# Output projection of a gated decoder layer: token-major in seven products, and the embedding projection moved ahead of the MLP

## The chip, the cores and the metric

One core of a Trainium2 chip. The metric is device time in microseconds (us) of one execution; "before" is the median of three runs, 952.14 us (951.76 to 952.27).

## The reference

One layer over 512 tokens with D = 1024: a normed input projection, gated linear attention and dilated attention side by side, then the part that matters here. Everything is float32.

```python
mix = (jax.nn.sigmoid(g_gla) * y_gla + jax.nn.sigmoid(g_att) * y_att) @ w_out[i]
x = x + mix
h2 = rmsnorm(x, ln2[i])
x = x + jnp.square(jax.nn.relu(h2 @ w_mlp1[i])) @ w_mlp2[i]
h3 = rmsnorm(x, ln3[i])
x = x + jax.nn.sigmoid(h3 @ w_pg[i]) * (p[i] @ w_pp[i])
return rmsnorm(x, ln_f)
```

`y_gla` ends with a product with `w_o_gla`; `p[i]` is a per-layer embedding, 512 tokens x 256, and `p[i] @ w_pp[i]` depends on nothing else in the layer.

## The kernel before

**Numbers and tiles.** Each float32 operand is split into a rounded part `hi` (ScalarE, a copy into float32r, `split_hi`) and a residual `lo` (VectorE, `split_lo`), and each 128 x 128 block of a product is three matmuls: hi x hi, hi x lo, lo x hi (`three`, L336). Tiles of 128 x 512 come from one pool of `NU` buffers: `u` (float32) and `ur` (hi or lo of an operand). PSUM has four banks `mmt` and four banks `smt`.

**Weights.** Every weight piece is 128 x 1024 (512 KB) and is one entry of `OPERANDS`, in the order of use. `fetch` (L301) runs ahead of TensorE: it issues the loads three operands ahead (`prepare`, L245: SyncE loads, and GpSimd a DMA that adds a second piece onto it in SBUF, L250), forms weight sums on VectorE (`sums`, L258), rounds to `hi` on ScalarE (L319) and takes the residual `lo` on VectorE (L297). At most `NRAW` = 8 raw pieces, five `hi` and four `lo` are held.

**Products.** A plain feature-major tile (`fm`, L346) is 8 K blocks x 3 = 24 matmuls of 512 columns. Most large products are done in Strassen-Winograd form: the two operands are cut in 2 x 2 blocks, and seven products of sums of blocks replace eight. `strassen` (L374) does so feature-major with 256 columns, `wide` (L416) token-major with 512: for each of the seven `WIDE` stages (weight sum A11, S1, S2, A12, S3, S4, A22 against operand sum B11, T1, T2, B21, T3, B22, T4) 24 matmuls into two of the banks. `begin` copies a bank out when a quarter's first part is ready, `end` adds the last part.

**Order.** Instructions stand on each engine in the order in which the Python code emits them. `run` (L330) emits n matmuls and then calls `step` (L220), which emits one pending closure of the list `later`, and from time to time a step of a generator in `side`. So vector and scalar work is woven between the matmuls, and a matmul that comes too early waits for it.

**The stages around the change.** `fm("og.j")` makes eight feature tiles of `y_gla` (L1276); VectorE multiplies by the gate and adds the attention branch into `tb[j]`, which is split into `mix[j]`. `fm("wo.j", mix)` makes eight feature tiles of the output projection (L1365), and VectorE adds each onto the transposed residual `xx[j]`, loaded by GpSimd (L1289, L1367). `x1_tile` scales by `ln2`, squares and sums for the norm, and forms the seven operand sums of the first MLP product. `stats` sums over partitions with one-column matmuls (L498), `to_tokens` turns `xx` into token-major tiles `x2` with 32 transposes (L1310, L1314); both run as `side` work during the first MLP product. The MLP is `m1q0` to `m1q7` (`strassen`, L374) and then `m2_plain` and `m2_seven`, which accumulate onto `x2` (L1455). `last_inputs` (L1498) loads the transposed embedding and ln_f when the S3 products of `m2_seven` end. Behind the MLP come `pp0`, `pp1` (`tmaj`, L353: 48 matmuls of 512 columns, copied out by ScalarE, L1577), the norm (L485, L486), and the gate `pg0`, `pg1`, which starts with token tile 0 and ends with the final norm and the stores.

Of the kernel before, what the change touches and what calls it, by code (L numbers as in the profile page):

```python
# [10 lines left out]
F32 = mybir.dt.float32  # L11
# [37 lines left out]
def weight_units():  # L49
# [39 lines left out]
    fm("wo", "w_out", 0, 8)  # L89
# [6 lines left out]
    for j in range(2):  # L96
        u.append((f"pp{j}.0", "tm", "w_pp", 0, j * 512))
# [56 lines left out]
def early():  # L154
    after_wide = False
    for n, i in OPERAND.items():
# [20 lines left out]
NU, NW, PIECE, WAYS = 67, 5, 8, 2  # L177
# [6 lines left out]

NWARM = 9
# [3 lines left out]
def block_kernel(ctx, tc, xT, ws, pT, wts, wha, wa2, vec, lnf, rel, onehot, ident_d, mask_d, out):  # L189
    nc = tc.nc  # L190
    V, S, TE, SY, GP = nc.vector, nc.scalar, nc.tensor, nc.sync, nc.gpsimd

    const = ctx.enter_context(tc.tile_pool(name="const", bufs=1))
# [64 lines left out]
    def sums(i):  # L258
        q, _, what = OPERANDS[i].partition(".")
        if q.startswith("m2c"):  # L260
# [40 lines left out]
    def fetch(upto):  # L301

        while done[0] < min(upto, len(OPERANDS) - 1):
            i = done[0] = done[0] + 1
            if i >= 0:
# [6 lines left out]
                if q.startswith("m2c") and what[:2] == "S2" and f"{q}.S4{what[2:]}" not in S4_LOADED:  # L312
# [33 lines left out]
    def fm(name, rhs, off=0, w=None, ps=None):  # L346
# [3 lines left out]
        run(three(ps, [(cols(w, slice(off + i * P, off + (i + 1) * P)), rhs[i]) for i in range(len(rhs))]))  # L350
        return ps

    def tmaj(name, n, lhs, evac, tts=range(4)):  # L353
# [3 lines left out]
        for tt in tts:  # L357
            ps = mmt()
            mms = three(ps, [(lhs(k, tt), cols(ready[f"{name}.{k // 2}"], slice((k % 2) * 512, (k % 2 + 1) * 512)))
                             for k in range(2 * n)])  # L360
            if tt < 3:
                run(mms)
            else:
                for i in range(n):
                    run(mms[6 * i:6 * i + 6])
# [50 lines left out]
    def wide(name, xo, finish):  # L416
# [4 lines left out]
        def begin(m, t, n, b):  # L421
            def go():
                sums[m, t, n] = u32()
# [6 lines left out]
        for i, (op, xname, b) in enumerate(WIDE):  # L430
# [3 lines left out]
            for pr in range(4):  # L434
# [8 lines left out]
                run(mms, 3, shared=True)  # L443
# [3 lines left out]
            if i in WEND:  # L447
                (m, t), b = WEND[i]
                later.extend(end(m, t, n, b) for n in range(2))
# [57 lines left out]
    def rms_gen(acc, res, wait=0, gap=0, squared=False):  # L507
# [15 lines left out]
        bc = const.tile([P, T], F32, tag="rstd", name="rstd", bufs=2)  # L523
# [751 lines left out]
    mix = [None] * KC  # L1275
    for j in range(KC):  # L1276
        py = fm(f"og.{j}", og)
        V.tensor_tensor(ga[j], py, ga[j], op=OP.mult)
        V.tensor_tensor(tb[j], tb[j], ga[j], op=OP.add)  # L1279
        if j < KC - 1:  # L1280
            split_later(tb[j], mix, j)
        else:
            mix[j] = split(tb[j])
    drain()

    xx = []
    for j in range(KC):
        t = u32()
        GP.dma_start(t, xT[j * P:(j + 1) * P, :])  # L1289
        xx.append(t)  # L1290

    acc1, norm2 = [], []
    x2 = {}

    def stats():
        for _ in range(30):
            yield
        r = rms_tok(acc1[0], True)
        n = const.tile([P, 4], F32, name="nrm2")
# [3 lines left out]
    def to_tokens():  # L1303
        for m in range(2):
            for t in range(2):
                pts = [smt() for _ in range(2)]
                for n in range(2):
                    tok = slice((2 * t + n) * P, (2 * t + n + 1) * P)
                    for i in range(4):
                        TE.transpose(pts[n][:, i * P:(i + 1) * P], xx[4 * m + i][:, tok], ident)  # L1310
                yield
                for n in range(2):
                    x2[m, t, n] = u32()
                    S.activation(x2[m, t, n], pts[n], AF.Copy)  # L1314
                yield

    blk, xop = [None, None], {}
    def operand(name, g, x):
        xop[name, g] = split(x)

    def x1_tile(j):

        x, c = xx[j], cv[:, C_LN2 + j:C_LN2 + j + 1]
        g, p, k = j // 4, j % 4 // 2, j % 2

        def first():
            if blk[g] is None:
# [419 lines left out]
```

## Time and profile before

| | |
|---|---|
| median of three runs | 952.14 us |
| profiled execution, its own time | 951.71 us |
| its span, first to last instruction | 949.6 us |
| TensorE matmuls (PE) | 941.3 us busy, 5892 records |
| VectorE (DVE) / ScalarE (ACT) / GpSimd (POOL) | 726.5 / 540.8 / 102.9 us busy |
| last matmul ends, after the span's start | 942.6 us |
| read from HBM / written | 143.03 MB / 8.17 MB |

The page lists for each engine its busy time, its share of the span and its instructions. A group's row reads: line, engine, operation, output <- inputs by tile names, shapes, count | busy us, mean ns of one | idle time of the engine just before them and what ended it. The rows of the chain are: start in us from the span's start, us, what. A timeline row is: start, us, engine, line, operation, tiles, shape, count. A matmul's own duration overlaps the next one's, so the pace is the distance from start to start. Lines after the change are those of the changed kernel.

### The profile page before, as it was taken

The numbers are of one execution on the slowest core, as the hardware profiler recorded it, in microseconds if no ns is written. First come the engines' busy times: TensorE is split into PE (matmuls) and PEld (weight loads), VectorE is DVE, ScalarE is ACT, GpSimd is POOL, SyncE is SP. The second block draws the span as 40 slices with busy tenths as digits, with TensorE's granted clock in tenths as the row PEclk, the third lists the DMA queues.
The fourth block names the chain that finished last, engine by engine and source line by source line (L and its number), as shares of the span: only waits on it lengthen the run. The fifth ranks groups of instructions, "written<-read, shape, count | busy, mean of one in ns | idle before, by whom it ended". The sixth has DMA issues, their size and how long they took to land.

```text
span 949.6 us, 15089 instructions
## 1 busy us (share of the span) xinstructions
PE 941.3 (99%) x5892; PEld 849.4 (89%) x5892; DVE 726.5 (77%) x1029; ACT 540.8 (57%) x880; POOL 102.9 (11%) x143
## 2 busy tenths in 40 slices
PE   9999999999999999999999999999999999999997
PEld 8789998899988888999988889999999888888886
DVE  7698879866789589878855788677777788988554
ACT  7357546445675479775732448555566445555643
POOL 0150010120100012022020000001000010020000
PEclk9999999999999999999999999999999999999999
DMA  9474482973818466456563436655647546796102
GB/s 352 142 236 114 129 201 68 289 234 100 200 46 227 159 144 182 132 134 200 156 199 92 131 89 173 154 142 134 162 129 191 141 100 166 218 306 222 53 0 89
DMA packets 46022, 150.34 MB, mean 158 GB/s; under 512 B 6723, under 2 KB 7311, under 8 KB 45952
## 3 DMA queue, kind: packets, MB, share of 16 engines
q1 hardware_dynamic: 29664, 100.61, 31.1%
q0 software_dynamic: 12608, 44.26, 23.5%
q10 hardware_dynamic: 3680, 4.51, 1.3%
q8 instruction: 46, 0.75, 0.3%
q14 instruction: 24, 0.20, 0.1%
HBM read 143.03 MB, written 8.17 MB: 159 GB/s over the span
## 4 chain that ended last, share of the span: by engine, by line
PE 98%; issue 1%; DMA 0%; ACT 0%; DVE 0%; POOLq 0%; POOL 0%; DVEq 0%
PE mmt L333 78%; PE smt L333 10%; PE mmt L581 2%; PE smt L1015 2%; PE smt L955 1%; PE smt L878 1%; PE smt L848 0%; PE smt L972 0%; PE smt L961 0%; PE smt L847 0%; PE smt L971 0%; PE smt L1310 0%; PE smt L1171 0%; PE smt L1071 0%; DMA cv<-in_vec_dram 0%
## 5 line engine op out<-in xcount | busy, mean ns | idle before, releaser
L333 PE MATMUL mmt<-ur,hi 128*128 128x256 f32 (+1 forms) x2320 | 476.0, 302 | 0.0
L333 PEld LDWEIGHTS mmt<-ur,hi 128*128 128x128 f32 x2320 | 373.1, 188 | 16.6
L333 PE MATMUL mmt<-ur,lo 128*128 128x256 f32 (+1 forms) x1160 | 351.2, 303 | 0.0
L297 DVE TENSOR_TENSOR lo<-w,hi 128x1024 fp32r<-128x1024 f32 x248 | 302.1, 1221 | 56.9 <-PE mmt L333 35.9
L319 ACT ACTIVATE hi<-w 128x1024 fp32r<-128x1024 f32 x248 | 259.2, 1054 | 93.8 <-PE mmt L333 24.5
L333 PE MATMUL mmt<-hi,ur 128*128 128x512 f32 (+3 forms) x832 | 241.1, 374 | 0.0
L333 PEld LDWEIGHTS mmt<-ur,lo 128*128 128x128 f32 x1160 | 218.6, 188 | 8.2
L333 PEld LDWEIGHTS mmt<-hi,ur 128*128 128x128 f32 x832 | 150.3, 188 | 25.7
L333 PE MATMUL mmt<-lo,ur 128*128 128x512 f32 (+3 forms) x416 | 154.8, 372 | 0.0
L461 ACT ACTIVATE ur<-u 128x512 fp32r<-128x512 f32 x111 | 66.1, 624 | 87.2 <-DVE u L1279 30.9
L333 PEld LDWEIGHTS mmt<-lo,ur 128*128 128x128 f32 x416 | 78.2, 188 | 13.6
L297 DVE TENSOR_TENSOR ur<-u,ur 128x512 fp32r<-128x512 f32 x110 | 72.7, 688 | 11.8 <-ACT ur L461 9.5
L333 PE MATMUL smt<-hi,ur 128*128 128x512 f32 x256 | 79.1, 390 | 0.0
L454 DVE TENSOR_TENSOR u<-u,mmt 128x512 f32<-128x512 f32 (+1 forms) x88 | 54.2, 647 | 26.9 <-PE mmt L333 26.6
L401 ACT ACTIVATE u<-mmt 128x512 f32<-128x512 f32 x72 | 43.1, 598 | 52.6 <-PE mmt L333 52.5
L250 POOL DMA_DIRECT2D w<-in_wts_dram x42 | 40.2, 1001 | 246.1 <-DMA w<-in_wts_dram 94.0
L333 PEld LDWEIGHTS smt<-hi,ur 128*128 128x128 f32 x256 | 47.8, 188 | 9.8
L276 POOL DMA_DIRECT2D w<-in_wts_dram x18 | 16.1, 894 | 317.9 <-DVE w L273 156.9
L333 PE MATMUL smt<-lo,ur 128*128 128x512 f32 x128 | 49.8, 389 | 0.0
L1389 ACT ACTIVATE u<-u 128x512 f32<-128x512 f32 x24 | 15.0, 628 | 26.7 <-DVE u L1385 26.7
L333 PEld LDWEIGHTS smt<-lo,ur 128*128 128x128 f32 x128 | 24.0, 188 | 5.0
L1250 ACT ACTIVATE u<-u 128x256 f32<-128x256 f32 x32 | 11.4, 411 | 20.9 <-DVE u L454 20.9
(235 smaller groups left out, 838.1 us busy)
## 6 DMA issues: line engine op xcount, KB each, us to landing
w<-in_wts_dram SPq DMA_DIRECT2D x180, 512.0 KB, 4.7
w<-in_wts_dram POOLq DMA_DIRECT2D x64, 512.0 KB, 6.8
u<-in_xT_dram SPq DMA_DIRECT2D x8, 256.0 KB, 5.3
u<-in_ws_dram SPq DMA_DIRECT2D x8, 256.0 KB, 5.4
v_dram<-u ACTq DMA_DIRECT2D x8, 256.0 KB, 6.6
u<-v_dram POOLq DMA_DIRECT2D x8, 256.0 KB, 6.2
y_dram<-u ACTq DMA_DIRECT2D x8, 256.0 KB, 2.0
u<-y_dram POOLq DMA_DIRECT2D x8, 256.0 KB, 6.2
```

The source lines that it names most:

```text
L250: GP.dma_start(w, wts[UNIT[b]], accum_op=OP.add)
L276: GP.dma_start(w, wts[UNIT[f"{q}.A21"]], accum_op=OP.add)
L297: V.tensor_tensor(lo, x, hi.bitcast(F32), op=OP.subtract)
L319: S.activation(hi[:, s], w[:, s], AF.Copy, scale=1.0 if c is None else c)
L333: TE.matmul(o, lhsT=l, rhs=r, start=a, stop=b, skip_group_check=shared)
L401: S.activation(sums[c], bank[b], AF.Copy, scale=-scale if c[0] else scale)
L454: V.tensor_tensor(out, s, ps, op=OP.subtract if m else OP.add)
L461: S.activation(hi, x, AF.Copy)
L581: TE.matmul(q0ps[i], lhsT=(hi, hi, lo)[j][:, c], rhs=(xh, xl, xh)[j], start=not k and not j, stop=k == KC - 1 and j == 2)
L1015: TE.matmul(o, lhsT=l[a][:, lc], rhs=r[b], start=start and i == 0, stop=stop and i == 2)
L1250: S.activation(outs[n], s[:, halves(n)], AF.Sigmoid)
L1389: S.activation(s, s, AF.Square)
```

## The change

The output projection `w_out` becomes token-major and goes through `wide` in seven products, with the gated mix as the operand that the sums are made of: `mix_even` and `mix_odd` form T1, T2, T4 and T3 tile by tile while the `w_o_gla` tiles are made, and split them. Its weight units become `quadw` pieces; S4 is made by a DMA that adds A12 onto S2 in SBUF (L319), as in the second MLP product. The residual x is read token-major: `begin_x` copies a bank to `x2` and has GpSimd add the x rows by DMA (L1378, L1379); the two tiles of the last product are loaded plainly (L1383). `onto_x` adds the final part. `x1_parts` transposes the `x2` tiles back to features (32 transposes, L1412) with ln2 applied in the copy out of PSUM (L1420); `x1_splits` forms and splits the operands of the MLP. The norm is taken from row sums of squares (L1392). `pp0` and `pp1` follow directly, and SyncE stores their eight tiles in DRAM (L1482, L1483); `last_inputs` reads them back (L1621). The gate then follows the MLP at once, with the token tiles in the order 2, 3, 0, 1. `NU` is 68 instead of 67.

```diff
-    fm("wo", "w_out", 0, 8)
+    quadw("wo", "w_out", (0, 512))
+    for j in range(2):
+        u.append((f"pp{j}.0", "tm", "w_pp", 0, j * 512))
...
-            EARLY.setdefault(i - 2, []).append((n, f"{q}.A11.{what[3:]}", f"{q}.A21.{what[3:]}"))
+            EARLY.setdefault(i - (5 if q == "wo" else 2), []).append((n, f"{q}.A11.{what[3:]}", f"{q}.A21.{what[3:]}"))
...
+        elif q == "wo" and what[:3] == "S4.":
+            return
...
-                if q.startswith("m2c") and what[:2] == "S2" and f"{q}.S4{what[2:]}" not in S4_LOADED:
+                if (q == "wo" or q.startswith("m2c")) and what[:3] == "S2." and f"{q}.S4{what[2:]}" not in S4_LOADED:
                     w = raw[f"{q}.S4{what[2:]}"] = raw[OPERANDS[i]]
                     GP.dma_start(w, wts[UNIT[f"{q}.A12{what[2:]}"]], accum_op=OP.add)
...
-                run(mms, 3, shared=True)
+                run(mms, 2 if base else 3, shared=True)
...
-        if j < KC - 1:
-            split_later(tb[j], mix, j)
-        else:
-            mix[j] = split(tb[j])
-    drain()
-
-    xx = []
-    for j in range(KC):
-        t = u32()
-        GP.dma_start(t, xT[j * P:(j + 1) * P, :])
-        xx.append(t)
+        later.extend((mix_odd if j % 2 else mix_even)(j // 2))
...
+    def begin_x(m, t, n, ps, sums):
+
+        o = sums[m, t, n] = x2[m, t, n] = u32()
+        S.activation(o, ps, AF.Copy, scale=-1.0 if m else 1.0)
+        GP.dma_start(o, x_rows(m, t, n), accum_op=OP.add)
...
+    for n in range(2):
+        x2[1, 0, n] = u32()
+        GP.dma_start(x2[1, 0, n], x_rows(1, 0, n))
...
+        for (m, t, n), x in sorted(x2.items()):
+            sq, c = u32(), 4 * m + 2 * t + n
+            S.activation(sq, x, AF.Square, scale=1.0 / 32.0, accum_out=ss[:, c:c + 1])
+            yield
...
+    def x1_ready(m, t):
+
+        res = [rest] * (3 if (m, t) == (1, 0) else 4) + x1_parts(m, t)
...
+        return res + x1_splits([("B11", 1), ("T1", 1), ("T4", 0), ("T4", 1), ("T2", 0), ("T2", 1), ("B21", 1),
+                                ("B22", 0), ("T3", 0), ("T3", 1)])
+
+    def onto_x(m, t, n, s, ps):
+        add(m, x2[m, t, n], x2[m, t, n], ps)
+        if n:
+            later.extend(x1_ready(m, t))
...
+            y = u32()
+            S.activation(y, ps, AF.Copy)
+            SY.dma_start(pp_dram[4 * j + tt], y)
...
-    for j in range(KC):
-        ps = fm(f"wo.{j}", mix)
-        V.tensor_tensor(xx[j], xx[j], ps, op=OP.add)
-        later.extend(x1_tile(j))
+    wide("wo", mix_op, onto_x, base=begin_x)
+    for j in range(2):
+        weight(f"pp{j}.0", 2 + j)
+        tmaj(f"pp{j}", 1, lambda k, tt: cols(pt[k], slice(tt * P, (tt + 1) * P)), evac_pp(j), piece=2, make=smt if j else mmt)
     side.append(stats())
-    side.append(to_tokens())
...
     def last_inputs():
-        for k in range(2):
+        for i in range(8):
             t = u32()
-            GP.dma_start(t, pT[k * P:(k + 1) * P, :])
-            pt.append(t)
+            GP.dma_start(t, pp_dram[i])
+            pps.append(t)
...
-    tmaj("pp0", 1, lambda k, tt: cols(pt[k], slice(tt * P, (tt + 1) * P)), evac_pp)
...
-    tmaj("pp1", 1, lambda k, tt: cols(pt[k], slice(tt * P, (tt + 1) * P)), evac_pp)
-    drain()
+    later.append(norm3)
...
-    tmaj("pg0", 4, x3_op, evac_pg0)
-    tmaj("pg1", 4, x3_op, evac_pg1, tts=range(3))
+    tmaj("pg0", 4, x3_op, evac_pg0, TTS, 4)
+    drain()
+    tmaj("pg1", 4, x3_op, evac_pg1, TTS[:3], last=-1)
```

More of the change, by code (lines that the diff above doesn't have):

```diff
@@ L448, in wide @@
                 (m, t), b = WEND[i]
-                later.extend(end(m, t, n, b) for n in range(2))
+                ends = [end(m, t, n, b) for n in range(2)]
+                if base:
+                    later[0:0] = ends
+                else:
+                    later.extend(ends)
     def add(m, out, s, ps, scale=1.0):
@@ L1562, in m2_seven @@
                 last_inputs()
-            elif (op, c) == ("A22", 2):
-                later.append(lambda: pt.__setitem__(slice(0, 2), [split(t) for t in pt]))
     pace[0] = 4608
@@ L1627, in scale_out @@
         S.activation(o, x2t[tt], AF.Copy, scale=fr[:, tt:tt + 1])
-        (S if tt == 3 else SY).dma_start(out[tt * P:(tt + 1) * P, 0:512], o)
+        (S if tt == TTS[-1] else SY).dma_start(out[tt * P:(tt + 1) * P, 0:512], o)
     def put(tt, c):
```

242 lines of the change are left out of this document (152 added, 90 removed).

## The prediction

> **What bounds the kernel now.** The page comes first, for the totals, the clock and the chain that ended last.
>
> ```profile
> span 949.6 us, 15089 instructions
> PE 941.3 (99%) x5892; PEld 849.4 (89%) x5892; DVE 726.5 (77%) x1029; ACT 540.8 (57%) x880; POOL 102.9 (11%) x143
> PEclk9999999999999999999999999999999999999999
> q1 hardware_dynamic: 29664, 100.61, 31.1%
> q0 software_dynamic: 12608, 44.26, 23.5%
> PE 98%; issue 1%; DMA 0%; ACT 0%; DVE 0%; POOLq 0%; POOL 0%; DVEq 0%
> ```
>
> TensorE is the chain: 98% of it, at a granted clock that never drops. A busy PE row is no proof of a full pipe, so I read the pace next, in the chain in order of time and, at the start and the end of the two output projections, in the timeline.
>
> ```profile
> 602.33 122.99 PE mmt L333 x1024
> 768.88 10.88 PE smt L333 x48
> 472.83 0.62 PE L333 MATMUL mmt<-ur,hi 128*128 128x512 f32 x2
> 559.88 0.41 PE L333 MATMUL mmt<-ur,hi 128*128 128x256 f32 x2
> ```
>
> The second row is 48 matmuls of 512 columns of a seven-product stage: 10.88/48 = 0.2267 us. The last two rows bracket w_o_gla and w_out, 2 x 8 tiles x 24 matmuls = 384: 87.05/384 = 0.2267 us as well. The first row gives 0.120 us for 256 columns. So TensorE never waits in the stretch that changes, and a matmul taken out is worth its 0.2267 us, as long as nothing new makes it wait. Every other engine has room: VectorE is busy 77% of the span, ScalarE 57%.
>
> **What TensorE loses and gains.** w_out had 8 tiles x 8 K blocks x 3 = 192 matmuls; seven products of 24 make 168. Gone: 24 x 0.2267 = **5.44 us**. Gone too are the four one-column sums of squares over partitions (L498, eight records), because the squares are now summed along each token's row by ScalarE:
>
> ```profile
> 601.38 0.95 PE L498 MATMUL smt<-ones,u 128*128 128x1 f32 x8
> 602.19 0.37 PE L333 MATMUL mmt<-ur,lo 128*128 128x256 f32 x1
> 602.40 0.40 PE L333 MATMUL mmt<-ur,hi 128*128 128x256 f32 x2
> 566.48 1.04 PE L1310 MATMUL smt<-ident,u 128*128 128x128 f32 x8
> ```
>
> 602.19 - 601.38 is 0.81, and the next matmul comes 0.21 instead of 0.12 later: **0.90 us**. The 32 transposes to tokens (four groups like the last row) go, and 32 transposes from tokens to features come, again in groups of eight: nothing. The 48 matmuls with the embedding move from behind the MLP to ahead of it: nothing. The sum is 5.44 + 0.90 = 6.34 us.
>
> The rest is whether the new cover holds. Durations for that, from the groups by form and from the instructions of single lines:
>
> ```profile
> L297 DVE TENSOR_TENSOR lo<-w,hi 128x1024 fp32r<-128x1024 f32 x248 | 302.1, 1221 | 56.9 <-PE mmt L333 35.9 <-ACT hi L319 11.1 <-issue 4.8
> L273 DVE TENSOR_TENSOR w<-w 128x1024 f32<-128x1024 f32 x18 | 22.1, 1226 | 0.6
> L297 DVE TENSOR_TENSOR ur<-u,ur 128x512 fp32r<-128x512 f32 x110 | 72.7, 688 | 11.8 <-ACT ur L461 9.5 <-ACT u L1250 1.4 <-DMA y_dram<-u 0.5
> L1278 DVE TENSOR_TENSOR u<-mmt,u 128x512 f32<-128x512 f32 x8 | 5.5, 692 | 19.0 <-PE mmt L333 19.0
> L609 DVE SCALAR_TENSOR_TENSOR u<-u 128x256 f32<-128x256 f32 x8 | 2.9, 422 | 0.0
> L454 DVE TENSOR_TENSOR u<-u,smt 128x512 f32<-128x512 f32 x6 | 3.8, 681 | 0.0
> L319 ACT ACTIVATE hi<-w 128x1024 fp32r<-128x1024 f32 x248 | 259.2, 1054 | 93.8 <-PE mmt L333 24.5 <-DVE w L279 11.8 <-issue 11.8
> L314 POOL DMA_DIRECT2D w<-in_wts_dram x4: 873/874/876, 774.7 to 797.7; - x4
> DMA to landing us min/median/max: 5.5/5.7/5.8
> L1289 POOL DMA_DIRECT2D u<-in_xT_dram x8: 543/633/899, 485.5 to 490.9; - x8
> DMA to landing us min/median/max: 7.6/8.5/10.1
> DMA to landing us min/median/max: 5.3/7.9/13.2
> ```
>
> The first landing row is L314's (weights added into SBUF, 512 KB, late in the MLP), the second L1289's (plain loads of x, 256 KB), the third L250's (adding weight loads, all stages).
>
> *VectorE at the third product.* In the orders, `w` is a raw weight tile, `hi` its rounding by ScalarE and `lo` the residual by VectorE; `u` is a tile of 512 columns, `ur` its rounding or residual. Before, VectorE at the seam between the projections has one weight residual per 5.4 us:
>
> ```order
> L1278 TENSOR_TENSOR u<-mmt,u 128x512
> L1279 TENSOR_TENSOR u<-u 128x512
> L297 TENSOR_TENSOR ur<-u,ur 128x512
> L297 TENSOR_TENSOR lo<-w,hi 128x1024
> L1367 TENSOR_TENSOR u<-u,mmt 128x512
> ```
>
> Now, from the end of the last w_o_gla tile (L1365) to the residual (`lo`) of S2's first half, the last row:
>
> ```order
> L1365 TENSOR_TENSOR u<-mmt,u 128x512
> L1366 TENSOR_TENSOR u<-u 128x512
> L302 TENSOR_TENSOR lo<-w,hi 128x1024
> L275 TENSOR_TENSOR w<-w 128x1024
> L302 TENSOR_TENSOR ur<-u,ur 128x512
> L622 SCALAR_TENSOR_TENSOR u<-u 128x256 x2
> L302 TENSOR_TENSOR ur<-u,ur 128x512
> L302 TENSOR_TENSOR lo<-w,hi 128x1024
> L275 TENSOR_TENSOR w<-w 128x1024
> L302 TENSOR_TENSOR ur<-u,ur 128x512
> L302 TENSOR_TENSOR lo<-w,hi 128x1024
> ```
>
> Three residuals, two weight sums and three operand splits now stand there: 2 x 0.69 + 3 x 1.221 + 2 x 1.226 + 3 x 0.688 + 2 x 0.422 = 10.4 us. TensorE wants that residual after A11 and S1 (48 matmuls) and two more: 50 x 0.2267 = 11.3 us. Slack 0.9 us if VectorE never waits; its waits for ScalarE's roundings can eat it. I count 0 to 2 us, and take 0.2.
>
> *The adding DMAs.* GpSimd loaded eight tiles of x in one go ahead of w_out, and they were needed only much later. Before, then after:
>
> ```order
> L1263 DMA u<-y_dram 128x512 x8
> L276 DMA w<-in_wts_dram 128x1024
> L250 DMA w<-in_wts_dram 128x1024
> L1289 DMA u<-in_xT_dram 128x512 x8
> L250 DMA w<-in_wts_dram 128x1024
> ```
>
> ```order
> L253 DMA w<-in_wts_dram 128x1024 x4
> L1383 DMA u<-in_x_dram 128x512 x2
> L319 DMA w<-in_wts_dram 128x1024
> L1379 DMA u<-in_x_dram 128x512 x2
> L319 DMA w<-in_wts_dram 128x1024
> L1379 DMA u<-in_x_dram 128x512 x4
> ```
>
> The first x addition (L1379) stands behind the addition that makes S4 (L319), which waits for the residual of S2: 10.4 us from the start of w_out. With 0.87 for L319 and 0.63 for the first x tile, the second is issued at 11.9. VectorE must add the fourth product onto both tiles (2 x 0.68), and TensorE transposes them after 4 x 24 + 14 = 110 matmuls, at 24.9 us. They must have landed by 24.9 - 1.4 = 23.5, 11.6 us after their issue. L1289's longest is 10.1, L250's 13.2: at the worst of these TensorE waits 1.6 us, at the medians (8.5 and 7.9) not at all. No row shows an adding DMA of 256 KB; I take the medians, and 0.1 us. S4's additions are issued at 10.4 and about 12.5 and read after 120 matmuls, at 27.2: even 13.2 leaves room for the rounding and the residual (1.05 + 1.22).
> The page "DMA: Bandwidth & Descriptors" of the Trainium skill (section "Anatomy of one DMA — SWDGE (gpsimd) path") gives 2.0 us plus bytes/436e3 for such a DMA, an estimate of 2.6 us here; by it this wait would be out of the question. The 8.5 us of L1289's row decides, so the wait stays in the range.
>
> *The first MLP quad.* Ten operand splits wait for the last x tiles and run during the embedding's 48 matmuls and the quad's first products. From the end of w_out to the residual of the quad's S2, VectorE has 19 instructions of 512 and 4 of 1024 columns: 19 x 0.688 + 4 x 1.221 = 18.0 us. TensorE needs it after 48 x 0.2267, the last eight transposes (0.87) and 74 x 0.120: 20.6 us. Slack 2.6 us; 0.1 us.
>
> *The queues that the stores and reloads pass.* Eight stores of the embedding's products go to SyncE's queue, each behind ScalarE's copy. The load of the quad's A12 stands behind three of them: it leaves about 4.7 us after w_out's end (18 matmuls and a copy), lands 4.7 later and is read at 23: hidden. Late in the MLP GpSimd reloads eight tiles instead of loading two, ahead of ln_f's two: ten issues of 0.9 us, begun four products (21.8 us) ahead of the gate.
>
> ```profile
> w<-in_wts_dram SPq DMA_DIRECT2D x180, 512.0 KB, 4.7
> u<-in_lnf_dram POOLq DMA_DIRECT2D x2, 256.0 KB, 12.0
> L1501 POOL DMA_DIRECT2D u<-in_pT_dram x2 | 1.5, 912 | 0.0
> L1577 ACT ACTIVATE u<-mmt 128x512 f32<-128x512 f32 x8 | 4.7, 594 | 2.7 <-PE mmt L333 2.7
> ```
>
> 9.1 + 12.0 = 21.1 us, and the first product is wanted a gate tile (5.4 us) later still: hidden. Only 2 MB more in each direction, spread over hundreds of us.
>
> *The end of the MLP.* Before, the 48 embedding matmuls (10.9 us) stood between the MLP's last product and the gate. Now the gate follows at once. ScalarE before, at that place, and then after:
>
> ```order
> L1483 ACTIVATE u,ss_7926<-u 128x512
> L1577 ACTIVATE u<-mmt 128x512
> L319 ACTIVATE hi<-w,cv 128x512 x4
> L1577 ACTIVATE u<-mmt 128x512 x3
> L461 ACTIVATE ur<-smt 128x512
> L1577 ACTIVATE u<-mmt 128x512
> ```
>
> ```order
> L474 ACTIVATE ur<-smt 128x512 x2
> L324 ACTIVATE hi<-w,cv 128x512 x8
> L1603 ACTIVATE u,ss_8074<-u 128x512 x2
> L1710 ACTIVATE u<-mmt,rt_9480 128x512
> L1721 ACTIVATE u,ss_9434<-u 128x512
> L474 ACTIVATE ur<-smt 128x512 x2
> ```
>
> The embedding's copies (L1577) are gone, and all roundings of the first gate half stand ahead of the last squares (L1603).
>
> ```profile
> L299 DVE SCALAR_TENSOR_TENSOR lo<-w,cv,hi 128x512 fp32r<-128x512 f32 x16 | 11.0, 750 | 3.2 <-ACT hi L319 3.2
> L1455 DVE SCALAR_TENSOR_TENSOR u<-mmt,nrm,u 128x512 f32<-128x512 f32 x4 | 2.9, 751 | 3.5 <-PE mmt L333 3.5
> L1483 ACT ACTIVATE u<-u 128x512 f32<-128x512 f32 x8 | 5.0, 629 | 8.3 <-DVE u L1455 8.3
> L486 POOL TENSOR_TENSOR rt<-rv,mh 128x4 f32<-128x4 f32 x1 | 1.5, 1508 | 47.8 <-DVE rv L485 47.8
> L1599 ACT ACTIVATE u<-mmt,rt 128x512 f32<-128x512 f32 x7 | 4.8, 685 | 9.5 <-PE mmt L333 9.5
> L461 ACT ACTIVATE ur<-u 128x512 fp32r<-128x512 f32 x111 | 66.1, 624 | 87.2 <-DVE u L1279 30.9 <-DVE u L609 14.6 <-DVE u L600 12.5
> ```
>
> Past the MLP's last matmul VectorE has only the fourth weight's residual left, 2 x 0.75 = 1.5 us, wanted 19 matmuls (4.3 us) on, and then the two last tile updates, to 3.0; their transposes come at 5.4. With the second square (0.63), small sums and the power (1.51) the norm is there at about 5.7, and it holds an evacuation, not TensorE. The last tiles belong to the first two token tiles, which the new order takes third and fourth: their splits are wanted at 2 x 5.44 + 0.9 + 12 x 0.2267 = 14.5 us. Ahead of them stand the first gate tile's evacuation, product, sum and square (0.69 + 2 x 0.69 + 0.63), and with two roundings and two residuals (2 x 0.62 + 2 x 0.69) they are through by about 11. Cost nothing; bound 0 to 6 us, the four weights' residuals in full (8 x 0.75).
>
> **The sum.** -6.34 + 0.2 + 0.1 + 0.1 = -5.94 us. The profiled execution took 951.71 us (its span 949.6 and 2.1 around it), so 945.8; the median is 0.43 us above it, so **946.2 us** beside 952.14.
>
> **The rivals.** In all of them the 6.34 us are gained; they differ in what is lost again.
>
> *VectorE and ScalarE become the bound around w_out and the first quad.* For it: slacks of 0.9 and 2.6 us against chains in which each split waits for a rounding and each weight sum for a residual. Against: the idle column of VectorE's commonest row is mostly waiting for TensorE. Two stalls of 1 to 2 us: 947.2 to 950. Chance 0.13.
>
> *The cover at the gate is missed.* For it: 10.9 us of other matmuls are gone from exactly there. Against: the loads counted above. Two to six us lost: 948 to 952. Chance 0.13. TensorE would then idle for once.
> The page "TensorE: Matmul & The Clock Gate" (Part 1, "The HAM clock gate") says that an idle window of about 3.4 us halves TensorE's clock for another window; a long stall would then cost an estimated 1.7 us more. No run here shows it, as the clock row has no dip.
>
> *Slower: w_out becomes bound by the DMA engines.* q1 moved 100.61 MB in 31.1% of the span, 341 GB/s; q0 44.26 MB in 23.5%, 198 GB/s. Between the start of w_out and the first transposes, 25 us, SyncE issues eight weight loads (4.2 MB, 12.3 us at q1's rate) and GpSimd four adding weight loads and six x tiles (3.7 MB, 18.5 us at q0's rate): 30.8 us of transfers. For it: that is more than 25. Against: only S4 and two x tiles must have landed by then. If adding x went at half of q0's rate (7.9 us more) and everything was served in order, TensorE would wait 38.7 - 25 = 13.7 us: 959.5. It decides from landings that are 8.2 us past the 11.6 above, about 20 us. Chance 0.07.
>
> *The change does not do what it says:* the matmuls go, but something else sets the end. With 98% of the chain on TensorE I give it nothing but the 0.02 that also holds gains beyond the count.
>
> **How the numbers follow.** Forecast 0.65 (945.2 to 947.2), VectorE 0.13, cover 0.13, DMA 0.07, other 0.02. The range takes the forecast with some 0.2 us below it and the first two rivals to their middles: 945.0 to 950.0; the DMA case and half of the cover case stay out. 0.2% is 1.9 us, about what a measurement of this kernel can tell from no change: faster means under 950.2. That holds the forecast, VectorE's case, half of the cover case and the rest: 0.86. Same is the cover case's other half, 0.07; slower the DMA case, 0.07.
>
> **What would show it.** Right: 28 matmuls fewer in the program; w_out from first to last product 168 x 0.2267 = 38.1 us and two groups of transposes; no gap of TensorE over 0.5 us there or at the gate; x additions landing in under 11.6 us. Wrong: a TensorE wait for `lo` at the third product or for x2's tiles at the first transposes, a dip in the clock row, or a gap where the gate begins.

## The result, and the profile after

Six runs of the changed kernel gave a median of 947.47 us (945.92 to 948.14), six of the kernel before, beside them, 952.2 us (950.77 to 952.6). The ratio is 0.995, with a 95% interval of 0.9937 to 0.9963: 4.7 us faster, by the intervals between 3.5 and 6.0. The forecast was 946.2. The profiled execution took 946.6 us against 951.71, its span 944.8 against 949.6.

The page of the changed kernel, the lines that answer to those of before:

```profile
span 944.8 us, 15151 instructions
PE 936.2 (99%) x5860; PEld 844.8 (89%) x5860; DVE 737.9 (78%) x1040; ACT 555.6 (59%) x918; POOL 113.2 (12%) x157
PEclk9999999999999999999999999999999999999999
q1 hardware_dynamic: 31104, 103.76, 31.6%
q0 software_dynamic: 14496, 49.51, 26.5%
PE 96%; issue 1%; DVE 1%; DMA 1%; ACT 0%; POOL 0%; POOLq 0%; DVEq 0%; ACTq 0%
```

TensorE has 32 records fewer: 24 matmuls and the eight records of the one-column ones. The chain is 96% TensorE instead of 98%: for some 19 us, up to 443.1, it runs through other engines, as the second list below shows. That is the length of the chain there, not time lost; TensorE lost 0.8 us.

The chain in order of time, first of the kernel before, then of the changed kernel (start, length, what):

```profile
469.19 92.78 PE mmt L333 x432
747.12 21.76 PE mmt L333 x96
```

```profile
428.79 6.82 DMA u<-y_dram
437.65 1.15 DVE lo L302
...
441.91 1.15 DVE lo L302
...
469.99 63.65 PE mmt L338 x296
...
569.93 161.29 PE mmt L338 x1344
...
753.02 21.76 PE mmt L338 x96
```

The first and the last of these TensorE pieces are the same places in both programs: the last gate weights with w_o_gla behind them, and the MLP's second plain half. Between them lie 277.93 us before. After, it is 283.03, but that holds the embedding's 48 matmuls, 10.88 us, which before came later: 272.15. The stretch of the change gained **5.78 us**, against 6.34 counted and 5.94 left in the forecast. But the changed kernel arrives 0.80 us later at its start, at a place where its program is still that of before. There, 0.64 us of start to start, lies TensorE's only wait for another engine behind the program's first microseconds. TensorE's waits in the changed kernel (who waited for whom, us of idle time in total, times, longest):

```profile
PE smt L566 <- POOL ones L561: 1.0, 1, 1.0
PE mmt L338 <- DVE lo L302: 0.5, 1, 0.5
```

The chain shows what led there: VectorE waits for a tile of y read back from DRAM, the residual of the next gate weight stands behind that tile's product in VectorE's order, and TensorE has to wait for that residual until 443.1.

The second thing to see is the x additions, in the row of line 1379, and the DMA share (all 16 engines) in most of w_out, first of the changed kernel, then of the kernel before (the columns are the stretch and its length, the busy time and count of PE, PEld, DVE, ACT and POOL, TensorE's clock, the DMA share and GB/s):

```profile
L1379 POOL DMA_DIRECT2D u<-in_x_dram x6: 864/1144/1430, 529.0 to 535.0; - x6
DMA to landing us min/median/max: 7.1/13.8/17.2
```

```profile
528.00:552.00 24.00, 24.00 (x115) 19.95 (x114) 16.63 (x19) 16.43 (x28) 8.31 (x10) 1.00 1.02 253
```

```profile
516.00:552.00 36.00, 36.00 (x161) 29.80 (x160) 25.16 (x40) 15.91 (x22) 0.91 (x1) 1.00 0.37 109
```

The forecast counted on 8.5 us to landing, from plain loads, and 7.9, from adding weight loads. The adding loads of x take 13.8 in the median and up to 17.2. The engines of the DMA are busy nearly all of these 24 us (share 1.02), where before they were at 0.37. TensorE lost only 0.04 us to it in this execution, because the second and third pair are needed later than the first. How near it came is what the experiments are about.

### The profile page after: what moved, and what is told of

Same layout as the page of the kernel before. It is cut to its first block, busy times and chain, and to the rows that moved or that the text cites. A ratio compares the mean times of both kernels' runs of the same rounds, so it can differ in the third digit from the quotient of the medians.

```text
span 944.8 us, 15151 instructions
## 1 busy us (share of the span) xinstructions
PE 936.2 (99%) x5860; PEld 844.8 (89%) x5860; DVE 737.9 (78%) x1040; ACT 555.6 (59%) x918; POOL 113.2 (12%) x157
## 4 chain that ended last, share of the span: by engine, by line
PE 96%; issue 1%; DVE 1%; DMA 1%; ACT 0%; POOL 0%; POOLq 0%; DVEq 0%; ACTq 0%
PE mmt L338 75%; PE smt L338 12%; PE mmt L594 2%; PE smt L1028 2%; DMA u<-y_dram 1%; PE smt L968 1%; PE smt L891 1%; PE smt L566 0%; PE smt L861 0%; PE smt L985 0%; PE smt L984 0%; PE smt L860 0%; PE smt L974 0%; PE smt L1412 0%; PE smt L1084 0%
## 5 line engine op out<-in xcount | busy, mean ns | idle before, releaser
L338 PE MATMUL mmt<-ur,hi 128*128 128x256 f32 (+1 forms) x2192 | 436.4, 297 | 0.0
L338 PEld LDWEIGHTS mmt<-ur,hi 128*128 128x128 f32 x2192 | 349.7, 189 | 11.8
L338 PE MATMUL mmt<-ur,lo 128*128 128x256 f32 (+1 forms) x1096 | 326.6, 298 | 0.5 <-DVE lo L302 0.5
L338 PE MATMUL mmt<-hi,ur 128*128 128x512 f32 (+3 forms) x912 | 266.2, 375 | 0.0
L338 PEld LDWEIGHTS mmt<-ur,lo 128*128 128x128 f32 x1096 | 206.6, 189 | 6.3 <-DVE lo L302 0.7
L338 PEld LDWEIGHTS mmt<-hi,ur 128*128 128x128 f32 x912 | 165.3, 188 | 28.6
L338 PE MATMUL mmt<-lo,ur 128*128 128x512 f32 (+3 forms) x456 | 170.6, 374 | 0.0
L338 PEld LDWEIGHTS mmt<-lo,ur 128*128 128x128 f32 x456 | 85.7, 188 | 15.1
L338 PE MATMUL smt<-hi,ur 128*128 128x512 f32 x288 | 89.1, 390 | 0.0
L844 ACT ACTIVATE u<-u,st 128x256 f32<-128x256 f32 (+1 forms) x32 | 15.6, 488 | 12.5 <-DVE st L840 11.0
```

Of the source, the lines that this page charges most:

```text
L338: TE.matmul(o, lhsT=l, rhs=r, start=a, stop=b, skip_group_check=shared)
L844: S.activation(q3[:, a, s:], q3[:, a, s:], AF.Exp, bias=nm[:, col + a:col + a + 1], accum_out=sums[:, col + a:col + a + 1])
```

## The experiments

My theory behind the comparison: the 24 matmuls are worth their pace and nothing that the change added holds TensorE, except that the adding loads land with almost no room, so that some executions lose up to 1.5 us to them; the stall at y is a chance of one execution. Rivals: VectorE, with the 0.9 us of slack of the prediction, is what is near its limit; the gate lacks its cover; the stall at y belongs to the change. Times are medians; each ratio is against the kernel before, run beside them.

**The matmuls alone.** In the kernel before:

```diff
-        ps = fm(f"wo.{j}", mix)
+        ps = fm(f"wo.{j}", mix[:KC - 1])
```

> The kernel before with the eighth K block of w_out left out (its product is missing from the sum): 24 matmuls of 512 columns fewer, nothing else. It prices the matmuls alone, without the new schedule. If TensorE alone sets the time: 24 x 0.2267 = 5.44 us less, 946.8. Rival (VectorE and ScalarE are close behind in this stretch and take part of it back): 947.5 to 950.

946.25 us (946.09 to 947.01, 5 runs), ratio 0.9941 (0.9928 to 0.9953): 5.75 us less. In its trace the chain from the same two places gives

```profile
469.92 87.34 PE mmt L333 x408
```

92.78 - 87.34 = 5.44 us, 24 x 0.2267 to the digit. Here too the start is late, by 0.73 us, in a kernel without the new schedule: 0.39 of it at the same residual of a gate weight, the rest in the program's first microseconds. The price of the matmuls is as forecast, and nothing around w_out took part of it back.

**The embedding back behind the MLP** (w_out stays in seven products; the embedding's products are kept in SBUF, so their stores and reloads are left out):

```diff
-    for j in range(2):
-        weight(f"pp{j}.0", 2 + j)
-        tmaj(f"pp{j}", 1, lambda k, tt: cols(pt[k], slice(tt * P, (tt + 1) * P)), evac_pp(j), piece=2, make=smt if j else mmt)
+    drain()
...
-    later.append(norm3)
+    tmaj("pp0", 1, lambda k, tt: cols(pt[k], slice(tt * P, (tt + 1) * P)), evac_pp)
+    norm3()
+    tmaj("pp1", 1, lambda k, tt: cols(pt[k], slice(tt * P, (tt + 1) * P)), evac_pp)
```

> The changed kernel with the embedding's 48 matmuls put back between the MLP and the gate, their products kept in SBUF (no stores, no reloads); w_out stays in seven products. My theory: the 48 matmuls are the cover of the first MLP quad, not of the gate. VectorE needs 18.0 us from the end of w_out to the quad's S2 residual; TensorE without the 48 matmuls wants it after 0.87 + 74 x 0.12 = 9.7 us, so it waits about 8.3 us there and gains nothing at the gate: 955.8. Rival (the cover was missed at the gate): putting it back gains up to 6 us there, 941.5 to 947.5. Third (neither place needs cover): 947.5.

956.9 us (956.16 to 957.65, 4 runs), ratio 1.0051 (1.0037 to 1.0065): 4.9 us slower than the kernel before, 9.4 slower than the changed one. TensorE's waits; the chain at the MLP's second half and at the end; and the same two rows of the chain of the changed kernel:

```profile
PE smt L1406 <- DVE u L467: 4.6, 5, 2.3
PE mmt L338 <- DVE lo L302: 4.0, 1, 4.0
```

```profile
731.65 21.79 PE smt L338 x96
...
945.92 4.79 issue
```

```profile
731.22 21.80 PE smt L338 x96
...
934.63 4.79 issue
```

Of 8.6 us of waiting, 4.0 are where I had put all of the loss, at the first quad's residual. The other 4.6 us I had not foreseen: they are at the transposes, for x tiles, whose adding loads land later still (8.9 to 22.4 us, median 16.5): the MLP's weights are now fetched in the same stretch, one adding load of them ahead of the third pair. Behind two of the waits TensorE's granted clock is 0.54 (563.6 to 567.0) and 0.50 (575.4 to 579.0), which costs some 4 us more, and the MLP's quicker pace, which two experiments below are about, gives 1.8 back. That the median comes near my 955.8 is partly luck. At the gate nothing is gained: from the MLP's second half to the end it is 945.92 - 731.65 - 10.88 (the 48 matmuls) = 203.39 us, against 934.63 - 731.22 = 203.41 in the changed kernel. The rival of the missed cover falls. The 48 matmuls ahead of the MLP are the cover without which the seven products lose.

**Four more sums on VectorE** between w_o_gla and w_out's first residuals:

```diff
+    for k in range(4):
+        V.tensor_tensor(ga[k], tb[0], tb[1], op=OP.add)
```

> The changed kernel with four more VectorE sums of 512 columns (results unused) between the last w_o_gla tile and w_out's first residuals: 4 x 0.69 = 2.75 us. In the trace of the changed kernel the residual of S2's first half ends 10.5 us after the start of w_out, and TensorE wants it at 11.3. If VectorE's slack there is the 0.9 us of the prediction: TensorE waits 1.85 us at the third product, the adding loads behind that residual go out 1.85 later, and nothing more is lost, since TensorE is later by as much: 949.3. Rival (VectorE has more room than its row of instructions shows): 947.5. Rival (the later adding loads miss their use as well): above 950.5.

949.3 us (948.4 to 951.83, 10 runs), ratio 0.9974 (0.9965 to 0.9983). The median is the one expected, 2.3 us above the changed kernel measured beside it (946.99, below). The profiled execution is the slowest of the ten, and says where time went:

```profile
PE smt L1415 <- DVE u L467: 2.1, 2, 1.8
PE mmt L338 <- DVE lo L302: 1.2, 1, 1.2
PE mmt L338 <- ACT u L1381: 0.4, 1, 0.4
```

1.2 for a residual and 0.4 behind it for a bank that ScalarE empties later: 1.6 us of idle time, 2.1 from start to start, where 1.85 was expected. But the residual is not the one that I had in mind. TensorE waits at w_out's 39th matmul (526.13), so for S1's second half; in the changed kernel that residual ends at 524.63 and is read at 525.77, a slack of 1.1 us, and the four sums start 0.60 apart, so they delay VectorE by 2.4 and not 2.75. When S2's first half is wanted, TensorE is already late, and the kernel does not test the 0.9 us of the prediction alone; it shows that VectorE has about 1 us here and not much more. The 2.1 us on top is x again, the second pair: the same weakness, hit from another side. The median shows little of it, so most executions will have lost less there; only this one has a trace.

**The adding loads, first try:** each x addition twice.

```diff
-        GP.dma_start(o, x_rows(m, t, n), accum_op=OP.add)
+        for _ in range(2):
+            GP.dma_start(o, x_rows(m, t, n), accum_op=OP.add)
```

> The changed kernel with every adding load of x (L1379) issued twice, twelve instead of six, so x is counted twice in three quarters of the tiles. In the trace of the changed kernel 2.5 MB of adding loads run from 528.2 to 552.2, 2.4 us for each 256 KB, and the tiles land 0.5 to 2.8 us ahead of their use. If adding loads are served one after the other at that rate: the first pair lands at 542.6 and TensorE waits about 1.9 us, the second at 557 (7.6 us more), the third at 566.6 (3.2 us more): 12.7 us in all, 960, between 956 and 962. Rival: the room is wide, since the software queue moves 198 GB/s while busy in the whole run (1.3 us for 256 KB) and lands everything by 549: 947.5 to 948.5, only GpSimd's issues more.

974.23 us (972.64 to 974.73, 4 runs), ratio 1.023 (1.0216 to 1.0244): a miss, 12 us above the top of what I expected. The second addition into a tile waits for the first to land, and all behind it in GpSimd's queue waits with it. Its landings are short (median 5.7 us) and its issues far apart, up to 575.8. So this kernel doubled a dependency as well as a load, and can't tell how fast the queue is. It shows something else, below.

**The adding loads, second try:** two additions more, into tiles that nothing reads.

```diff
+        if (m, t, n) == (0, 0, 0):
+            for k in range(2):
+                GP.dma_start(ga[k], x_rows(k, 1, 1), accum_op=OP.add)
         GP.dma_start(o, x_rows(m, t, n), accum_op=OP.add)
```

> The changed kernel with two more adding loads of x (256 KB each, into two tiles that nothing reads any more) in GpSimd's queue ahead of the first x addition. In the trace of the changed kernel the adding loads land one after the other at about 2.4 us for 256 KB, so every later one lands 4.8 us later: the first pair at 542.7, VectorE's two sums then end at 544.1, and the transposes that came at 542.1 wait 2.0 us; the second pair at 551.8, transposes ready at 552.5 and wanted at 550.9: 1.6 more; the third pair at 557, in time. In all 3.6 us: 951.1. Rival (an adding load costs 1.3 us of its queue, 256 KB at 198 GB/s): landings 2.6 later, waits of 0 and about 1.6: 949. Rival (room enough): 947.5.

952.12 us (950.87 to 952.82, 10 runs), ratio 1.0003 (0.9993 to 1.0012): the whole gain is gone, for two loads of 256 KB. The row of the x additions and TensorE's transposes in the timeline (in brackets the idle time ahead and what ended it):

```profile
DMA to landing us min/median/max: 11.5/18.4/20.0
```

```profile
541.97 0.33 PE L1415 MATMUL smt<-ident,u 128*128 128x128 f32 x1
544.60 0.98 PE L1415 MATMUL smt<-ident,u 128*128 128x128 f32 x7 [2.30 <-DVE u L467]
554.15 0.33 PE L1415 MATMUL smt<-ident,u 128*128 128x128 f32 x1 [1.05 <-DVE u L467]
554.75 0.98 PE L1415 MATMUL smt<-ident,u 128*128 128x128 f32 x7 [0.27 <-DVE u L467]
```

The first pair makes TensorE wait 2.3 us where 2.0 was expected, the second 1.3 where 1.6 was. These 3.6 us are the sum expected; the median is 5.1 above the changed kernel beside it, and the last section shows 1.6 us more behind the first wait. An adding load of 256 KB costs its queue about 2.4 us in this stretch, against 1.3 by the whole run's rate of q0, and there was no room for two.

**What runs beside them:** the first load for the MLP's first S1 weight two operands later (and the y products moved, as below).

```diff
-            EARLY.setdefault(max(i - (4 if after_wide else 6), 0), []).append((n, f"{q}.A21", f"{q}.A22"))
+            EARLY.setdefault(max(i - ((2 if q == "m1q0" else 4) if after_wide else 6), 0), []).append((n, f"{q}.A21", f"{q}.A22"))
```

> The kernel with the three products with y behind the residual, and the first load for the MLP's first S1 weight (with its adding load) two operands later, so that fewer transfers run beside the x additions. In the kernel with the y products moved, the second pair of x tiles landed at 546.3 where VectorE could have added it earlier, and TensorE waited 0.17 us at the second group of transposes. If DMA traffic sets that: the second and third pair land 1 to 2.5 us sooner, no wait at that group, span 943.9 to 944.1, median 946.2 to 946.6. Rival: the adding queue's own pace sets the landings, whatever else runs: same landings, 946.6.

947.17 us (946.46 to 948.79, 5 runs), ratio 0.9952 (0.994 to 0.9965). The x additions, and the row of the stretch with its DMA share:

```profile
DMA to landing us min/median/max: 7.1/14.2/17.6
```

```profile
528.00:552.00 24.00, 23.74 (x114) 19.59 (x113) 16.65 (x19) 16.00 (x26) 7.71 (x10) 1.00 1.02 248
```

Landings and share (1.02) are those of the changed kernel, and TensorE still waits 0.26 us at the second group of transposes. Moving one transfer did not empty the stretch, since others took its place. So the run does not test its theory: whether the adding queue has a pace of its own or the full engines set it stays open.

**Fewer adding loads:** S4 as a VectorE sum of two tiles that are in SBUF.

```diff
-        elif q == "wo" and what[:3] == "S4.":
-            return
...
-                if (q == "wo" or q.startswith("m2c")) and what[:3] == "S2." and f"{q}.S4{what[2:]}" not in S4_LOADED:
+                if q.startswith("m2c") and what[:3] == "S2." and f"{q}.S4{what[2:]}" not in S4_LOADED:
```

> The changed kernel with w_out's S4 weights made as S2's are, by VectorE (S2 plus A12, both in SBUF), instead of by an adding load of A12 from DRAM: two adding loads of 512 KB fewer in GpSimd's queue ahead of the x additions, two VectorE sums of 1.23 us more, in the stretch where VectorE is idle 1.3 and 0.8 us in the trace of the changed kernel. In that trace and its repeat the adding loads landed at 2.4 to 2.6 us for 256 KB, and the second pair of x tiles 0 to 1.1 us too late, with waits of TensorE of 0.05 and 1.55 us. If the adding queue is what costs: the first pair lands about 5 us sooner, the second and third about 9 us, no wait at the transposes, and the median falls by 0.3 to 1.0 below the 947.0 to 947.5 of the changed kernel: 946.0 to 947.0. Rival (the two sums make VectorE late for a residual): a wait of 0.5 to 2.5 us on lo, 947.5 to 949.5.

945.71 us (945.46 to 946.16, 5 runs), ratio 0.9935 (0.9921 to 0.9948). The same two views:

```profile
DMA to landing us min/median/max: 4.0/6.9/10.4
```

```profile
528.00:552.00 24.00, 24.00 (x116) 20.04 (x115) 19.73 (x23) 16.82 (x27) 5.97 (x7) 1.00 0.85 221
```

The x tiles land in half the time, the engines of the DMA are less full (0.85), and TensorE waits for none of it; the two sums (VectorE 19.73 us of these 24 instead of 16.63) find room. The median is 1.3 to 1.8 us below the two series of the changed kernel (947.47, and 946.99 below); each against the kernel before beside it, the gain is 6.0 instead of 4.7 and 4.9. The five runs lie within 0.7 us, where the two series of the changed kernel span 2.2 and 2.0. That fits a wait that hangs on landings, but it is weak evidence, since the kernel before spans 0.7 to 2.6 us in its own series, and the ratios' intervals overlap. The traces say more: from start to start, four with S4's adding loads, the changed kernel twice and the two with the y products moved, lose 0.04, 1.6, 0.2 and 0.5 us at the second group of transposes, and the three with VectorE sums, this one and two below, lose nothing. On average that is 0.6 us; why the medians differ by more is not shown.

**The stall at y:** first the changed kernel once more, then with the first three products with y (L1279) behind the residual.

> The changed kernel, unaltered, once more, beside the kernels of this group. If the 0.6 us that TensorE waits at 443.1 for VectorE hangs on when y's second tile happens to land (a tile of 256 KB that landed 1 us later than in the kernel before, whose program is the same up to there), this execution shows another amount, 0 to 0.7 us, and the median stays at 947.5 within 0.6. Rival: the wait belongs to the change, and stands there again at 0.6.

```diff
-    later.extend(merge(j) for j in range(KC))
+    later.extend([lambda: None] * 3 + [merge(j) for j in range(KC)])
```

> The changed kernel with one order altered: on VectorE the first three products with y (L1279, read back from DRAM) stand behind the weight residual that follows them instead of ahead of it; the other four engines are as they were. In the trace of the changed kernel VectorE waits at 434.7 for the second y tile, the residual behind it ends at 438.8 instead of the 437.7 of before, and TensorE waits 0.6 us at 443.1. If that order is what lost the 0.6 us: no wait of TensorE there, span 944.2, median about 946.9 (947.47 less 0.6). Rival: the late y tile was the chance of one execution and the stall is not in most runs: 947.5, no change. Third: the product moved back now makes a later wait, 947.5 to 948.5.

The repeat: 946.99 us (945.78 to 947.75, 5 runs), ratio 0.9947 (0.9934 to 0.9959). No stall at y, but the second pair of x tiles late; TensorE's waits there are

```profile
PE smt L1412 <- DVE u L467: 1.1, 2, 0.9
PE smt L566 <- POOL ones L561: 1.0, 1, 1.0
```

With the products moved: 946.57 (945.96 to 947.38, 5 runs), ratio 0.9944 (0.9931 to 0.9958), and no stall at y either. The wait at y stands in one of the traces of the changed kernel and not in the other, and a smaller one (the matmul that reads the residual starts 0.28 us late) in the kernel before with 24 matmuls fewer. It is a chance of executions of both kernels, and the gain of 0.6 that I expected of the move can't be claimed. Up to w_o_gla TensorE's order of work is the same in all fourteen traces of this document, and w_o_gla begins between 472.7 and 473.6 in them; the three without the change alone cover 472.8 to 473.6. A kernel with both repairs, the VectorE sums for S4 and this move:

> The same, and the first three products with y behind the residual that follows them. If both stalls (0 to 0.6 us at y, 0 to 1.5 at the second pair of x tiles) are taken away, TensorE does not wait from 445 on: span 943.8 to 944.1, median 945.8 to 946.5, below both kernels. Rival (the sums cost VectorE what the queue gains): 946.6 or more.

946.0 us (945.6 to 946.51, 5 runs), ratio 0.9937 (0.9924 to 0.9949): below both kernels, as expected, and no better than with the VectorE sums alone.

**The one-column matmuls alone**, in the kernel before:

```diff
-        r = rms_tok(acc1[0], True)
+        r = const.tile([P, 4], F32, name="rtok", bufs=3)
+        V.tensor_scalar(r, acc1[0][:, 0:4], EPS, None, op0=OP.add)
+        V.reciprocal(r, r)
```

> The kernel before without the four one-column matmuls that sum the squares over partitions (L498); the norm is then taken from unsummed squares, so that part of the computation is left out. By the prediction they cost TensorE 0.90 us (0.81 in their rows, and the next matmul 0.21 later instead of 0.12). By the two traces side by side it is 0.70: the 208 matmuls ahead of them run at 0.1190 instead of 0.1200 in the count of starts, which gives 0.20 back. Start of the gate in the trace 0.70 or 0.90 sooner; median 951.1 to 951.3.

949.49 us (949.3 to 950.33, 9 runs), ratio 0.9977 (0.9968 to 0.9987): 2.2 us, well over either number that I had expected. The chain of this kernel, then a row of the chain of the kernel before, whose next is the one of 1024 matmuls in the prediction:

```profile
576.88 146.20 PE mmt L333 x1232
```

```profile
576.86 24.68 PE mmt L333 x208
```

146.20/1232 = 0.1187 us a matmul, from the last transposes to the end of the quads. Before, the 208 ahead of the one-column matmuls ran at 24.68/208 = 0.1187 too, and the 1024 behind them at 122.99/1024 = 0.1201. The matmuls taken out had cost 0.81 us and, behind them, 1024 x 0.0014 = 1.4. And in the changed kernel, 161.29/1344 = 0.1200: without the one-column matmuls it still runs at the slower pace.

**Transposes ahead of the MLP.** In all traces the quicker pace follows transposes. So, in the kernel with the VectorE sums:

```diff
+    turned = smt()
+    for i in range(4):
+        TE.transpose(turned[:, i * P:(i + 1) * P], x2[0, 0, 0][:, i * P:(i + 1) * P], ident)
     for q in range(8):
         quad(q)
```

> The kernel whose S4 weights are VectorE sums, with four transposes of 128 columns (their product unused) between the embedding's last matmul and the MLP's first. In all traces 256-column matmuls that follow transposes run at 0.1187 us each; in the kernel before the MLP runs at 0.1187 up to the four one-column matmuls and at 0.1200 behind them; without these it keeps 0.1187 to its end; and in the changed kernel, where 512-column matmuls lead straight into the MLP, all 1344 run at 0.1200. If what stands directly ahead of the stream sets its pace for as long as nothing else comes between: 1344 x 0.0013 = 1.75 us less, the transposes cost 0.4, and an order of 1.3 us is gained: span 942.5, median 944.3. Rival (the pace hangs on something else in the MLP's own order, the buffers or the time since an idle stretch): 0.1200 as before and 0.4 us for the transposes, 946.1.

944.41 us (944.17 to 944.96, 5 runs), ratio 0.9924 (0.991 to 0.9937): its slowest run is below the fastest, 945.46, of the kernel it was made from.

```profile
569.08 0.44 PE smt L1566 x4
569.51 159.49 PE mmt L336 x1344
```

159.49/1344 = 0.1187, where that kernel has 161.29 as the changed one. Four transposes that compute nothing, 0.44 us, bring back 1.8. This is the fastest kernel of the study, 7.4 us below the kernel before.

## Why the prediction was right, point by point

The sum held in sign and nearly in size: 4.7 us measured where 5.9 were forecast, and the median lies inside the range. Of the missing 1.2, the stretch of the change accounts for 0.16 (5.78 against 5.94) in the profiled execution; the rest is the stall at y there, and in the repeat waits for x. The other executions have no trace. That 5.78 is so near 5.94 is partly luck: of the 0.4 us of waits that I took off, only 0.04 came, and the pace of the matmuls, for which the sum has no term, took 0.5.

- *24 matmuls, 5.44 us.* Right, shown alone.
- *The one-column matmuls, 0.90, and transposes for transposes, 0.* Together I put 0.90; the traces give 0.34 for the two (5.78 - 5.44). This is the term that was mis-sized: I took one pace, 0.120 us, for all matmuls of the MLP, and so a group of transposes as worth the same wherever it stands. In both programs the matmul behind a group starts the next about 0.09 us late, in the changed kernel 0.32 later instead of 0.23, and before 0.20 instead of 0.12, as these rows of the two timelines show:

```profile
542.88 0.48 PE L338 MATMUL mmt<-lo,ur 128*128 128x512 f32 x1
543.20 0.62 PE L338 MATMUL mmt<-hi,ur 128*128 128x512 f32 x2
```

```profile
562.60 0.36 PE L333 MATMUL mmt<-ur,hi 128*128 128x256 f32 x1
562.80 0.27 PE L333 MATMUL mmt<-ur,lo 128*128 128x256 f32 x1
```

  Before, that was paid back: the 304 matmuls behind the four groups ran at 0.1187 instead of 0.1200, 0.40 us in all, about as much as the four late starts and the one behind the one-column matmuls together. So the MLP's 1344 matmuls take 161.3 us in both programs, before without its transposes and one-column matmuls, and of the 0.90 only the 0.81 of the rows was gained. Among matmuls of 512 columns nothing is paid back: the four groups cost 0.10 to 0.12 us more each there, 0.44 in all, and 0.04 went to x at the second one: 0.81 - 0.48 = 0.33, within 0.01 of what was measured. What the change could have gained, 1344 x 0.0013 = 1.8 us, it did not, since its 512-column matmuls lead straight into the MLP.
- *VectorE at the third product: slack 0.9.* Right, to a tenth, in the trace of the changed kernel. w_out begins at 517.16, the residual of S2's first half ends at 527.6, and TensorE takes it at 528.5:

```profile
517.16 0.62 PE L338 MATMUL mmt<-hi,ur 128*128 128x512 f32 x2
...
526.41 1.22 DVE L302 TENSOR_TENSOR lo<-w,hi 128x1024 fp32r<-128x1024 f32 x1
...
528.49 0.39 PE L338 MATMUL mmt<-lo,ur 128*128 128x512 f32 x1
```

- *x additions, 0.1, "x additions landing in under 11.6 us".* Right for the first pair (7.1 and 8.4 us) and wrong as a statement on all. I worked out one deadline, the first pair's, with the durations of plain loads and of adding loads elsewhere in the run; I also counted two groups of transposes inside w_out, and there are three. Here the six stand in line with two more of 512 KB: the second pair took 12.7 and 14.8, the third 15.1 and 17.2. The repeat waited 1.1 us for the second pair, the first execution lost 0.04. The slower rival, "w_out becomes bound by the DMA engines", pointed the right way with its 30.8 us of transfers for 25, and was given 0.07 because only two tiles had to have landed by then. The DMA engines were indeed nearly full for 24 us. It did not decide, but two loads more took the whole gain; it deserved a closer look at each deadline.
- *The first MLP quad: slack 2.6.* No wait, as forecast; the embedding's matmuls cover it, shown by taking them away.
- *The gate: nothing.* Right, shown: with the cover put back, this part is 0.02 us shorter.
- *The stall at y* was no part of the prediction and not of the change either.

## What to carry to other kernels

A transfer that replaces an engine's work gets a deadline for each tile, and its time to landing is read from a stretch as full of transfers as the new one will be, not from the run's average. Two transfers fewer in the right place gave 1.1 to 1.3 us, each kernel against the one before beside it. And the price of a small instruction on the engine that bounds includes the pace of the stream behind it: divide long rows of the chain by their counts, those ahead of the instruction as well as those behind it.

## What the runs showed of the hardware that was not expected

- **Two paces for the same matmul.** 256 columns take 0.1187 us behind transposes and 0.1200 behind one-column or 512-column matmuls, and keep the pace for over a thousand matmuls. Four transposes switch it. The granted clock is 1.00 in both (603 to 725 us in the changed kernel and in the one with four transposes). In the kernel with the embedding put back, transposes stand directly ahead of the MLP too, and from 600 to 700 us it runs at 0.1187, though TensorE waited 4.0 us in between. Why is not shown.
- **Half pace after a short wait.** In the kernel with two more additions, after 2.30 us of idle time, matmuls of 512 columns start 0.43 apart for 3.2 us. The last row below is the stretch from 545.7 to 549.0; its PEclk, third from the end, says that TensorE was granted half its clock:

```profile
546.87 1.06 PE L338 MATMUL mmt<-hi,ur 128*128 128x512 f32 x2
547.72 0.63 PE L338 MATMUL mmt<-lo,ur 128*128 128x512 f32 x1
```

```profile
545.70:549.00 3.30, 3.30 (x9) 2.56 (x8) 0.26 (x1) 1.35 (x2) 0.00 (x0) 0.50 1.08 301
```

  Its first wait thus cost some 1.6 us more than its length, and the three of the kernel with doubled additions about 2 each. Waits of 1.84 and 0.27 us, one transpose apart, in the kernel with four more sums did the same (granted clock 0.54 from 553.5 to 557.2). After waits of 0.88 and 0.27 us in the repeat, and of 1.41 and 0.27 in the kernel with the embedding put back, the pace held. The page "TensorE: Matmul & The Clock Gate" of the Trainium skill (Part 1, "The HAM clock gate") gives half the clock after an idle window of about 3.4 us, for about as long; the half agrees with these rows, and the length with this kernel's 3.2 us, while here waits of 2.3 and of 1.84 and 0.27 us were enough. After the 4.0 us of the kernel with the embedding put back, the half pace lasted longer, 5.4 us (575.4 to 580.8).
- **Adding loads of 256 KB** landed 2.4 to 2.6 us apart while the DMA engines were full, about 105 GB/s; the first in its queue, with S4's adding loads gone, landed 4.0 us after its issue.
